# Six of the eight x pieces of the lower half asked for together, into landing tiles and idle sweep tiles

## The chip, the core and the metric

The kernel runs on one core of a Trainium2 chip. The metric is the device time of one execution in microseconds (us). TensorE does the matmuls, VectorE (DVE), ScalarE (ACT) and GpSimd (POOL) the elementwise work, and SyncE (SP) and ScalarE issue the DMAs, which run on 16 DMA engines that the queues share. Each engine works through its own instructions strictly in order.

## What is computed

One layer of a hybrid encoder on 2048 tokens of width 1024, all in float32. Only its first step, the combined input projection, is touched by the change:

```python
u = _rms_norm(h, norm_mix_g[l])
proj = u @ w_in[l]
hy = _short_conv_centred(proj[..., :HY_COLS], hy_conv_w[l], hy_conv_b[l])
...
qk = jax.nn.silu(_short_conv_centred(proj[..., HY_COLS:off], ml_conv_w[l], ml_conv_b[l]))
```

`h` is x here. The columns of `proj` are the input of the Hyena group (1536 columns, a long convolution by FFT), q and k of an mLSTM (1024), its v and output gate (1024) and its scalar gates (16). After both groups come an output projection, cross-attention into 256 memory tokens, a squared-ReLU MLP and a last norm.

## The kernel before

**Products.** A float32 operand is split into a high and a low part (`split`, L367: ScalarE casts the high part, VectorE subtracts it from the source to get the low one), and a product is made of three matmuls (`mm3`, L355). The left operand of the projection lives in two tiles for the whole stage: `xh` and `xl`, 128 partitions by 8 blocks of the width by 1024 tokens. That is one half of the tokens. There is one pair of these tiles, so the halves take turns in them.

**Pieces of x.** A half is two token chunks of 512, and a chunk is loaded in four pieces (c, j) of two width blocks: `x_load` (L517), 128 x 1024 elements each, from the transposed x, issued by SyncE into a landing tile of the tag "xn", of which there are two. `scaled` (L512) then does for a piece: two gains on VectorE (L510: times the norm's gain, times the row of inverse root mean squares `rb`), the cast into `xh` on ScalarE and the subtraction into `xl` on VectorE (L368). A chunk's `rb` is made by `diagonal` (VectorE, L496) and `spread` (a matmul with ones, L502, and a copy, L506). `x_chunk` (L524) is the generator that does this for one chunk, asking for piece j + 1 just ahead of `scaled` of piece j; `prep_x` (L639) chains the generators of both chunks of a half into `prepq`, and `pop` (L624) advances it by one piece.

**Who uses x.** Two kinds of passes over the weight columns, both 256 wide:

- `sweep` (L719) computes columns transposed, for the convolutions: each column block has two row tiles m and two token chunks, copies the products into a tile "P" (128 x 1088, two of them), convolves into a tile "cv" (the same size, two of them), and `sweep_out` (L789) transposes and stores the result.
- `natural` (L834) computes columns with the tokens on the partitions: for each weight tile eight row tiles t of 128 tokens. Row tiles 0 to 3 read token chunk 0 of the half, 4 to 7 chunk 1. It stores v and the sigmoid of o (L859) by ScalarE's queue (L860) and the gates by SyncE's (L865). It uses no "P" and no "cv".

**The order around the change.** `program` (L2019) lays out: sweeps 0 to 3 over half 0, then half 1 into `xh` and `xl` (`prep_x(1)`), sweeps 0 to 9 and `natural(1, (3, 0, 1, 2))` over half 1, then half 0 again (`prep_x(0)`, the "lower half" in what follows, since its rows come second), `natural(0, (3,))`, sweeps 4, 5, 8 and 9, and so on. Inside the last weight tile of `natural(1, ...)`, at row tile 4, `after()` sets `prepq`. From there on each row tile pops one piece: the four of chunk 0 in row tiles 4 to 7 of that weight tile (whose matmuls no longer read chunk 0), the four of chunk 1 in row tiles 0 to 3 of `natural(0, (3,))`, and its row tiles 4 to 7 need them.

The whole sequence is woven by `weave` with the generators of Hyena (`hyena`, L867), which run on TensorE between the projection's matmuls. In this stretch Hyena reads `a<-zg` (L935) and `a<-hy` (L938) by SyncE's queue, 1.5 MB for each step.

**Who sets the order on the engines.** The program text gives priorities and dependences. The order that each engine gets comes from a planner that simulates a time line (`schedule_with_timeline_sim`, L1988): it lets an instruction or a DMA go ahead of its place in the text when its inputs and its tile are free in the simulated time. The real engines then keep that order, so an instruction that waits holds everything behind it on its engine, and a DMA that waits holds everything behind it in SyncE's or ScalarE's queue.

Of the kernel before, what the change touches and what calls it, by code (L numbers as in the profile page):

```python
# [10 lines left out]
F32 = mybir.dt.float32  # L11
# [9 lines left out]
D = 1024  # L21
# [112 lines left out]
class Prog:  # L134
# [386 lines left out]
        self.nc.sync.dma_start(out=t, in_=src[:, 2 * j:2 * j + 2, 512 * c:512 * c + 512])  # L521
        return t

    def x_chunk(self, c):  # L524
        rb = self.spread(self.diagonal(self.rx[:, 4 * c:4 * c + 4]))
        xs = [self.x_load(c, 0)]
        for j in range(4):
            if j < 3:
                xs.append(self.x_load(c, j + 1))
            to = slice(2 * j, 2 * j + 2), slice(512 * (c % 2), 512 * (c % 2) + 512)  # L530
            self.scaled(xs.pop(0), 2 * j, self.g_mix, rb, *(t[(slice(None),) + to] for t in (self.xh, self.xl)))
            yield

    def x_first(self):
        nc, sb = self.nc, self.isb
# [101 lines left out]
        yield  # L637

    def prep_x(self, hf):  # L639
        self.prepq = chain(self.x_chunk(2 * hf), self.x_chunk(2 * hf + 1))  # L640

    def prep_mem(self):
        sb = self.isb
# [190 lines left out]
    def natural(self, hf, tiles, after=None, at=4):  # L834
        nc, a, sb = self.nc, self.a, self.isb
        xh, xl = self.xh, self.xl
        win = a["w_in"][0]
        for c2 in tiles:
            n = 256 if c2 < 3 else 272
            c0 = 2560 + 256 * c2  # L840
            wh, wl = next(self.wst)
            for t in range(8):
                if t % 4 == 0:
                    yield 11
                if t == at and c2 == tiles[-1] and after is not None:
                    after()
                ts = slice(128 * t, 128 * t + 128)
                r0 = 1024 * hf + 128 * t
                p = self.mm()
                for k in range(8):  # L850
                    self.mm3(p[:, :n], xh[:, k, ts], xl[:, k, ts], wh[:, k, :n], wl[:, k, :n], k == 0, k == 7)
                if self.pending:
                    self.pending.pop(0)()
                self.pop()
                so = sb.tile([128, 512], F32, tag="st", name="st", bufs=3)[:, 0:256]
                if c2 < 2:
                    nc.scalar.copy(so, p[:, :256])
                else:
                    nc.scalar.activation(so, p[:, :256], AF.Sigmoid)  # L859
                nc.scalar.dma_start(out=(self.d_vd if c2 < 2 else self.d_od)[r0:r0 + 128, 256 * (c2 % 2):256 * (c2 % 2) + 256],  # L860
                                  in_=so)
                if c2 == 3:
                    sg = sb.tile([128, 16], F32, tag="sg", name="sg", bufs=2)
                    nc.vector.tensor_tensor(sg, p[:, 256:272], self.gb, ALU.add)
                    nc.sync.dma_start(out=self.d_gt[r0:r0 + 128], in_=sg)  # L865
# [1130 lines left out]
def chain(*gens):  # L1996
    for g in gens:
        yield from g


def weave(a, b, wa, wb, until=False):
    da = db = 0.0
    fa = fb = False
    while not (fa and fb):
        if fb or (not fa and da / wa <= db / wb):
            try:
                da += next(a)
            except StopIteration:
                fa = True
        else:  # L2010
            try:
                db += next(b)
            except StopIteration:
                fb = True
                if until:
                    return


def program(p):  # L2019
    with ExitStack() as ms:  # L2020
        with ExitStack() as es:
            p.inproj_open(es)
            p.filters_open()
            p.prepq = p.x_first()
            p.pop()
            s = chain(p.sweep(range(4), 0, True, lambda: p.prep_x(1)), p.opened(), p.sweep(range(4), 1, False))
            f = p.filters()
            for _ in range(5):
                next(s)
            next(f)  # L2030
            next(f)
            next(s)
            weave(s, f, 140, 102, True)
            p.gates_open(es)
            n = p.memproj()
            m = p.mlstm(ms)
            with ExitStack() as hs:
                rest = chain(s, p.sweep(range(4, 10), 1, True), p.natural(1, (3, 0, 1, 2), lambda: p.prep_x(0)),
                             p.natural(0, (3,)), among(p.sweep((4, 5, 8, 9), 0, False), p.gates(), 2),
                             among(chain(p.natural(0, (0, 1)), p.sweep((6, 7), 0, False),  # L2040
                                         p.natural(0, (2,), p.prep_mem, 2)), p.states(), 1),
                             p.turned_in(), take(n, 2), beside_each(n, take(m, 6)))
                weave(rest, p.hyena(hs), 499, 297, True)
            for _ in rest:
                pass
        with ExitStack() as rs:
            p.ts = rs.enter_context(ExitStack())
            p.tail_open(p.ts)
            with ExitStack() as at:
                g = p.attention(at)  # L2050
                weave(g, m, 440, 96, True)
                ms.close()
                p.ffn_open(rs)
                for _ in g:
                    pass
            p.ffn()


def among(g, h, every):
    for i, v in enumerate(g):  # L2060
        yield v
        if i % every == every - 1:
            next(h, None)
    for _ in h:
        pass


def beside_each(g, h):
    for v in g:
        yield v  # L2070
        yield next(h, 0)
    yield from h


def take(g, n):
    for _ in range(n):
        v = next(g, None)
        if v is None:
            return
        yield v  # L2080
# [31 lines left out]
```

## Time and profile before

| | |
|---|---|
| median of 3 runs | 3120.02 us (3117.74 to 3126.49) |
| the profiled execution's own time | 3121.71 us |
| its span, first to last instruction | 3120.0 us |
| TensorE busy | 3025.7 us, 97% |
| mean granted TensorE clock | 0.988 |
| DMA moved | 607.07 MB, 195 GB/s on average |

All times of the trace are in microseconds from the span's start. A row of a timeline names the start, the length, the engine, the line, the operation, the tile written <- the tiles read, and in brackets the idle time before it and what ended it. SPq and ACTq are the DMA issues of SyncE and ScalarE. A row of a table of stretches gives, for each engine, its busy time and the number of instructions, then the granted TensorE clock (1.00 is full), the busy share of the DMA engines and what they moved. A list of waits names who waited for whom, the total in us, how many times, and the longest.

### The profile page before, as it was taken

How to read it: one execution, taken by the hardware profiler on the slowest of the kernel's cores; microseconds unless marked ns; L12 is line 12 of the kernel's file. 1: busy time of each engine (PE TensorE's matmuls, PEld its weight loads, DVE VectorE, ACT ScalarE, POOL GpSimd, SP SyncE). 2: the span in 40 equal slices, each digit the busy share in tenths (PEclk: the TensorE clock that was granted, in tenths of full speed). 3: DMA queues.
4: the chain of work that ended last, by engine and by line, in shares of the span. 5: the costliest groups of instructions: out<-in, count | busy, mean ns of one | idle time of the engine just before them, and what ended most of it. 6: DMA issues, size and time to landing. Idle time of an engine off the chain costs nothing.

```text
span 3120.0 us, 42912 instructions
## 1 busy us (share of the span) xinstructions
PE 3025.7 (97%) x14257; PEld 2374.8 (76%) x14257; DVE 1957.9 (63%) x3428; ACT 1498.4 (48%) x2930; POOL 1145.9 (37%) x802
## 2 busy tenths in 40 slices
PE   8999999989999898999999999999999999999998
PEld 6655667766677666888888888887888888888876
DVE  7865465446747356777665656657555686565696
ACT  6543465533646225555544455556455443333335
POOL 0122011200223243233142337766455475242693
PEclk9999999999999998999999999999999999999999
DMA  6554767676877996455375657656644565353434
GB/s 212 189 197 163 231 211 219 177 237 199 252 209 241 277 321 228 140 197 179 130 268 191 212 168 240 202 180 227 202 152 151 169 216 183 112 166 113 161 92 172
DMA packets 444102, 607.07 MB, mean 195 GB/s; under 512 B 38494, under 2 KB 248542, under 8 KB 442856
## 3 DMA queue, kind: packets, MB, share of 16 engines
q1 hardware_dynamic: 405988, 546.54, 54.3%
q10 hardware_dynamic: 37892, 57.79, 5.4%
q8 instruction: 113, 1.85, 0.2%
q14 instruction: 109, 0.89, 0.1%
HBM read 401.79 MB, written 202.41 MB: 194 GB/s over the span
## 4 chain that ended last, share of the span: by engine, by line
PE 55%; DVE 2%; issue 1%; DMA 1%; ACT 0%; POOL 0%; SPq 0%; ACTq 0%; POOLq 0%; DVEq 0%
PE mm L357 12%; PE mm L360 12%; PE mm L361 12%; PE hy L361 6%; PE hy L357 6%; PE hy L360 6%; DVE bl L1631 1%; PE hy L1287 1%; PE hy L1289 1%; DVE acc L1923 0%; PE hy L1534 0%; DVE acc L1957 0%; PE hy L1423 0%; DMA e<-hg 0%; PE hy L1249 0%
## 5 line engine op out<-in xcount | busy, mean ns | idle before, releaser
L1630 ACT CAST ah<-w 128x512 fp32r<-128x512 f32 x284 | 176.6, 622 | 304.8 <-PE hy L360 157.8
L1631 DVE TENSOR_TENSOR bl<-wr,bh 128x512 fp32r<-128x512 f32 x213 | 242.2, 1143 | 124.8 <-ACT bh L1630 124.2
L368 DVE TENSOR_TENSOR wl<-wn,wh 128x512 fp32r<-128x512 f32 (+1 forms) x300 | 220.6, 781 | 100.1 <-ACT wh L368 99.5
L998 POOL TENSOR_TENSOR b<-b,a 128x512 f32<-128x512 f32 x64 | 87.2, 1365 | 514.5 <-ACT b L996 215.4
L357 PE MATMUL mm<-xh,wh 128*128 128x512 f32 x640 | 267.5, 419 | 8.6 <-ACT wh L368 8.0
L360 PE MATMUL mm<-xl,wh 128*128 128x512 f32 x640 | 253.8, 397 | 1.3 <-DVE xl L368 1.3
L361 PE MATMUL mm<-xh,wl 128*128 128x512 f32 x640 | 255.0, 399 | 0.0
L1630 ACT CAST bh<-wr 128x512 fp32r<-128x512 f32 x232 | 143.5, 621 | 230.3 <-PE mm L361 173.1
L1631 DVE TENSOR_TENSOR al<-w,ah 128x512 fp32r<-128x512 f32 x236 | 216.8, 919 | 56.1 <-ACT ah L1630 56.0
L361 PE MATMUL mm<-bh,al 128*128 128x512 f32 x576 | 223.7, 391 | 2.6 <-POOL al L1631 2.6
L357 PE MATMUL mm<-bh,ah 128*128 128x512 f32 x576 | 225.6, 392 | 0.1
L360 PE MATMUL mm<-bl,ah 128*128 128x512 f32 x576 | 225.1, 391 | 0.0
L368 ACT CAST wh<-wn 128x512 fp32r<-128x512 f32 (+1 forms) x300 | 166.6, 618 | 113.9 <-PE mm L361 51.8
L360 PE MATMUL mm<-act,wh 128*128 128x512 f32 x512 | 200.6, 392 | 0.8 <-DVE act L368 0.8
L357 PE MATMUL mm<-act,wh 128*128 128x512 f32 x512 | 198.9, 394 | 1.4 <-ACT wh L368 1.3
L361 PE MATMUL mm<-act,wl 128*128 128x512 f32 x512 | 199.0, 392 | 0.0
L357 PE MATMUL hy<-bh,ah 128*128 128x512 f32 x448 | 175.2, 391 | 0.0
L360 PE MATMUL hy<-bl,ah 128*128 128x512 f32 x448 | 174.6, 390 | 0.0
L361 PE MATMUL hy<-bh,al 128*128 128x512 f32 x448 | 174.4, 390 | 0.0
L357 PEld LDWEIGHTS mm<-xh,wh 128*128 128x128 f32 x640 | 121.2, 190 | 60.9 <-issue 18.6
L357 PE MATMUL mm<-wh,xh 128*128 128x256 f32 (+1 forms) x512 | 155.2, 304 | 12.6 <-ACT xh L368 10.2
L361 PEld LDWEIGHTS mm<-xh,wl 128*128 128x128 f32 x640 | 121.0, 189 | 47.9 <-issue 23.2
(371 smaller groups left out, 8217.9 us busy)
## 6 DMA issues: line engine op xcount, KB each, us to landing
wr<-hc SPq DMA_DIRECT2D x224, 256.0 KB
w<-in_ff_w_dram SPq DMA_DIRECT2D x172, 256.0 KB
hc<-wn SPq DMA_DIRECT2D x128, 256.0 KB
wn<-in_w_in_dram SPq DMA_DIRECT2D x100, 256.0 KB
hc<-q SPq DMA_DIRECT2D x96, 256.0 KB
fs<-a SPq DMA_DIRECT2D x32, 512.0 KB
a<-fs SPq DMA_DIRECT2D x64, 256.0 KB
a<-zs SPq DMA_DIRECT2D x64, 256.0 KB
```

The source lines that it names most:

```text
L357: first = mm(ps, lh, rh, start=start, stop=False)
L360: mm(ps, lh, rl, start=False, stop=False)
L361: self.last = mm(ps, ll, rh, start=False, stop=stop)
L368: both = (self.nc.scalar.copy(hi, src), self.nc.vector.tensor_tensor(lo, src, hi.bitcast(F32), ALU.subtract))
L998: nc.gpsimd.tensor_tensor(xt, xt, hi[:, m], ALU.mult)
L1287: nc.tensor.matmul(dst, nm[:, h], va[:, h], start=True, stop=state is None)
L1289: nc.tensor.matmul(dst, rows_[d, 1][:, h], state[:, h], start=False, stop=True)
L1630: self.nc.scalar.copy(hi, src)
L1631: eng.tensor_tensor(lo, src, hi.bitcast(F32), ALU.subtract)
```

## The change

`x_chunk` and the chain of two are replaced by one generator over all eight pieces of a half, `x_chunks(hf)`. When it is called it first issues `deep` loads: two for half 1, six for half 0. Of the six the first two land in "xn" as before, and pieces 2 to 5 in tiles of the tags "P" and "cv", two of each. After each piece's `scaled` the load of the piece `deep` places further on is issued, into "xn": for half 0 these are the last two pieces. For half 1 a load now follows the `scaled` that frees its tile in the text, where it stood ahead of it, and the loads of the second chunk no longer stand behind that chunk's `spread`.

In `natural` the value `True` for `after` now stands for this generator: it is made (and so its loads are asked for) at row tile 0 of the last weight tile, and put into `prepq` at row tile 4, where the pieces began before. What is computed does not change, and neither does the number of loads, gains, casts and subtractions.

```diff
-    def x_chunk(self, c):
-        rb = self.spread(self.diagonal(self.rx[:, 4 * c:4 * c + 4]))
-        xs = [self.x_load(c, 0)]
-        for j in range(4):
-            if j < 3:
-                xs.append(self.x_load(c, j + 1))
-            to = slice(2 * j, 2 * j + 2), slice(512 * (c % 2), 512 * (c % 2) + 512)
-            self.scaled(xs.pop(0), 2 * j, self.g_mix, rb, *(t[(slice(None),) + to] for t in (self.xh, self.xl)))
-            yield
+    def x_chunks(self, hf):
+        parts = [(2 * hf + i, j) for i in range(2) for j in range(4)]
+        deep = 2 if hf else 6
+
+        def room(n):
+            if not 1 < n < deep:
+                return None
+            t = self.isb.tile([128, 1088], F32, tag=("P", "cv")[n % 2], name="xt", bufs=2)
+            return t[:, 0:D].rearrange("p (k t) -> p k t", k=2)
+
+        xs = [self.x_load(*parts[n], room(n)) for n in range(deep)]
+
+        def steps():
+            rb = None
+            for n, (c, j) in enumerate(parts):
+                if j == 0:
+                    rb = self.spread(self.diagonal(self.rx[:, 4 * c:4 * c + 4]))
+                to = slice(2 * j, 2 * j + 2), slice(512 * (c % 2), 512 * (c % 2) + 512)
+                self.scaled(xs.pop(0), 2 * j, self.g_mix, rb, *(t[(slice(None),) + to] for t in (self.xh, self.xl)))
+                if n + deep < 8:
+                    xs.append(self.x_load(*parts[n + deep]))
+                yield
+        return steps()
...
     def prep_x(self, hf):
-        self.prepq = chain(self.x_chunk(2 * hf), self.x_chunk(2 * hf + 1))
+        self.prepq = self.x_chunks(hf)
...
                 if t % 4 == 0:
                     yield 11
-                if t == at and c2 == tiles[-1] and after is not None:
-                    after()
+                if c2 == tiles[-1] and after is not None:
+                    if after is True and t == 0:
+                        nxt = self.x_chunks(0)
+                    if t == at:
+                        if after is True:
+                            self.prepq = nxt
+                        else:
+                            after()
...
-                rest = chain(s, p.sweep(range(4, 10), 1, True), p.natural(1, (3, 0, 1, 2), lambda: p.prep_x(0)),
+                rest = chain(s, p.sweep(range(4, 10), 1, True), p.natural(1, (3, 0, 1, 2), True),
```

## The prediction

> **What bounds the kernel now.** I began with the first part of the page, then read the list of who waited for whom on TensorE over the whole span (columns: who waited <- for whom; us in total, times, longest).
>
> ```profile
> span 3120.0 us, 42912 instructions
> PE 3025.7 (97%) x14257; PEld 2374.8 (76%) x14257; DVE 1957.9 (63%) x3428; ACT 1498.4 (48%) x2930; POOL 1145.9 (37%) x802
> ```
>
> ```profile
> PE mm L696 <- ACT o L686: 11.3, 2, 10.1
> PE mm L357 <- ACT xh L368: 10.2, 2, 7.4
> ```
>
> TensorE is busy for 97% of the span, so what can be won without removing matmuls are its gaps, 94.3 us in all. The second largest entry is the one that the change can reach: matmuls of L357 that wait for the cast of x (L368) twice, 7.4 us at the longest. Where this is, TensorE's timeline shows (start, us, engine, line, what, and in brackets the idle time before it and who ended it):
>
> ```profile
> 640.48 0.29 PE L357 MATMUL mm<-wh,xh 128*128 128x272 f32 x1
> ...
> 657.99 0.59 PE L191 MATMUL hy<-a,f 64*128 64x512 f32 x1
> 666.02 0.59 PE L357 MATMUL mm<-wh,xh 128*128 128x272 f32 x1 [7.44 <-ACT xh L368]
> ...
> 672.33 0.39 PE L357 MATMUL mm<-wh,xh 128*128 128x272 f32 x1 [0.86 <-DVE sg L864]
> ...
> 674.39 0.39 PE L361 MATMUL mm<-wh,xl 128*128 128x272 f32 x1 [0.24 <-DVE xl L368]
> ...
> 683.41 0.39 PE L357 MATMUL mm<-wh,xh 128*128 128x272 f32 x1 [2.72 <-ACT xh L368]
> ...
> 686.78 0.40 PE L357 MATMUL mm<-xh,wh 128*128 128x512 f32 x1
> ```
>
> The matmuls with 272 columns from 640.48 are the lower half's first weight tile, `natural(0, (3,))`. Its first four row tiles read token chunk 0, its last four chunk 1. TensorE stops at 658.58, when only chunk 1 is left to do. The four gaps sum to 7.44 + 0.86 + 0.24 + 2.72 = 11.26 us. Slices of 5 us there add the clock (columns: stretch; length and TensorE; weight load; VectorE; ScalarE; GpSimd; granted clock; DMA share; GB/s):
>
> ```profile
> 660.00:665.00 5.00, 0.00 (x0) 0.00 (x0) 0.87 (x2) 0.73 (x3) 0.00 (x0) 0.66 1.05 284
> 665.00:670.00 5.00, 3.98 (x14) 3.32 (x16) 3.75 (x5) 1.46 (x2) 0.00 (x0) 0.50 0.77 226
> 670.00:675.00 5.00, 3.90 (x21) 2.21 (x18) 2.66 (x6) 1.82 (x3) 0.00 (x0) 0.81 1.01 335
> ...
> 680.00:685.00 5.00, 2.28 (x16) 1.85 (x15) 2.64 (x3) 1.04 (x1) 0.00 (x0) 1.00 0.31 103
> ```
>
> After the 7.44 us gap the work ran at a clock of 0.50 and then 0.81: 3.98 x 0.50 + 3.90 x 0.19 = 2.7 us lost. After the 2.72 us gap it stayed at 1.00. So the switch costs 11.26 + 2.7 = 13.96 us, and that is the most to be won there.
>
> Why x is late, VectorE, ScalarE and SyncE's queue tell in turn:
>
> ```profile
> 631.85 2.73 DVE L510 SCALAR_TENSOR_TENSOR xt<-xt,par,rb 128x512 f32<-128x512 f32 x4
> ...
> 640.09 1.42 DVE L510 SCALAR_TENSOR_TENSOR xt<-xt,par,rb 128x512 f32<-128x512 f32 x2 [3.17 <-DMA xt<-in_x_t_dram]
> ...
> 645.09 2.49 DVE L368 TENSOR_TENSOR wl<-wn,wh 128x512 fp32r<-128x512 f32 x4
> ...
> 650.91 1.29 DVE L1013 TENSOR_TENSOR a<-hy,a 128x512 f32<-128x512 f32 x2 [1.80 <-DMA a<-hy]
> ...
> 657.60 1.41 DVE L510 SCALAR_TENSOR_TENSOR xt<-xt,par,rb 128x512 f32<-128x512 f32 x2 [4.33 <-DMA xt<-in_x_t_dram]
> ```
>
> ```profile
> 633.29 1.05 ACT L368 CAST xh<-xt 128x1024 fp32r<-128x1024 f32 x1 [0.53 <-DVE xt L510]
> ...
> 661.97 0.33 ACTq L860 DMA_DIRECT2D od<-st  x1
> 662.40 0.66 ACT L859 ACTIVATE st<-mm 128x256 f32<-128x256 f32 x2 [9.34 <-DMA a<-zg]
> ...
> 664.93 1.04 ACT L368 CAST xh<-xt 128x1024 fp32r<-128x1024 f32 x1 [1.87 <-DMA wn<-in_w_in_dram]
> ```
>
> ```profile
> 152.58 11.71 SPq L521 DMA_DIRECT2D xt<-in_x_t_dram  x4
> ...
> 635.74 1.59 SPq L521 DMA_DIRECT2D xt<-in_x_t_dram  x2
> ...
> 647.96 0.39 SPq L521 DMA_DIRECT2D xt<-in_x_t_dram  x1
> ...
> 648.90 2.22 SPq L935 DMA_DIRECT2D a<-zg  x2
> ...
> 656.60 0.37 SPq L521 DMA_DIRECT2D xt<-in_x_t_dram  x1
> ...
> 667.26 0.38 SPq L521 DMA_DIRECT2D xt<-in_x_t_dram  x1
> ...
> 674.37 0.38 SPq L521 DMA_DIRECT2D xt<-in_x_t_dram  x1
> ```
>
> Piece (0,2) of chunk 0 is 3.17 us late, under cover of other matmuls. Two things hold the first piece of chunk 1. Its load went out at 647.96, because both landing tiles ("xn") were full until then, and VectorE got it at 657.60. Its gain was done at 659.0, yet the cast came at 664.93: ScalarE stood 9.34 us at an `od` store (L860), behind the landing of Hyena's `a<-zg`, on DMA engines that were full (share 1.05). The later pieces come one by one behind each other's tiles: 656.60, 667.26, 674.37.
>
> **The change part by part.** *Six pieces at once.* Of the eight loads of the lower half, six go out from 635 on. The other two are among the four of 152.58, 480 us before VectorE takes them up at 631.85: the planner issues a load as soon as its tile is free, whatever the place in the program. So the two in "xn" don't move. Four pieces now land in the sweeps' "P" and "cv" tiles, and pieces 7 and 8 take the freed "xn" tiles, at 635.74, where (0,2) and (0,3) went before. The loads of 647.96, 656.60, 667.26 and 674.37 leave the crowded stretch.
>
> *What then paces the switch.* One piece costs VectorE 1.41 (two gains, 657.60) and 1.23 for xl (shortest, median and longest in ns):
>
> ```profile
> L368 DVE TENSOR_TENSOR xl<-xt,xh x8: 1212/1226/1226, 634.5 to 683.4; 128x1024 fp32r<-128x1024 f32 x8
> ```
>
> Eight pieces take 8 x 2.64 = 21.1 us; with 2.49 for the weights and 1.29 for Hyena, VectorE would be through at 631.85 + 24.9 = 656.7, before TensorE gets to 658.58. ScalarE needs 8 x 1.05 (633.29) = 8.4 us for the casts. So the data can be there in time; all 13.96 us are open to be won. The bounds of what stays: 0 where the casts stand ahead of the blocked store in ScalarE's order, and 6.0 where they stand behind it (worked out as the first rival). I take 2.0, nearer to 0: with data at hand the cast followed its gain after 0.53 us at 633.29, and the planner, to which x is now there, has no reason to put three stores ahead.
>
> *The clock.* It comes back with the gap. The rows say that 2.72 us keep it and 7.44 lose it. The Trainium skill, "TensorE: Matmul & The Clock Gate", Part 1, puts the limit at an idle window of about 3.4 us; both rows agree with it, and by it a remaining gap of 2 us would cost no clock.
>
> *The four loads in their new place.* "P" and "cv" come free when the last sweep of the upper half is written out:
>
> ```profile
> 483.28 1.26 DVE L773 SCALAR_TENSOR_TENSOR cv<-P,par,cv 128x1008 f32<-128x1008 f32 x1
> ...
> 510.95 0.60 SPq L832 DMA_DIRECT2D kn<-st  x1
> ...
> 490.00:515.00 25.00, 23.53 (x130) 17.22 (x129) 18.01 (x29) 19.01 (x32) 8.31 (x6) 1.00 0.93 284
> 515.00:535.00 20.00, 20.00 (x120) 15.98 (x119) 8.33 (x19) 9.59 (x20) 2.05 (x2) 1.00 0.42 115
> ...
> xt<-in_x_t_dram SPq DMA_DIRECT2D x6, 512.0 KB
> ```
>
> The first "P" is read for the last time at 484.5, the last `kn` store of the second "cv" goes out at 510.95. As the planner pulled the two loads of 152.58, I expect the four in 484 to 512, 120 us before their use. 4 x 0.524 MB at 284 GB/s are 7.4 us of DMA, in a stretch with a share of 0.93, ahead of one with 0.42. Lower bound 0: TensorE's gaps of 490 to 515 sum to 1.47 us, and the loads of a stage run ahead of it. Upper bound: four loads held SyncE's queue for 11.71 us at 152.58; held like that, and with the 7.4, what is behind them comes 19.1 us late. What that hold cost TensorE is seen in its waits from 140 to 180:
>
> ```profile
> PE hy L191 <- DVE b L338: 1.3, 1, 1.3
> PE mm L360 <- DVE xl L368: 1.3, 1, 1.3
> ```
>
> None of it is laid to a late load. I take 1.0. (The Trainium skill, "DMA: Bandwidth & Descriptors", Queues, rings and completion order, says that each DMA engine takes one queue's descriptors in ring order; by it, loads pulled ahead delay every SyncE load behind them by their whole 7.4 us, and the sum would come out 6.4 us higher. No row here shows which share of such a delay reaches TensorE.)
>
> *The upper half.* With two landing tiles its loads go out when "xn" is freed, as now; the loads of the second chunk only lose their place behind `spread`. The wait it has is the 1.3 us on xl above; VectorE's work sets it. 0, within -1.3 to +1.3.
>
> *The sweeps' tiles.* The lower half's first sweep needs "P" at 686.78, some 30 us after the gains are through; 0, covered by `natural`'s matmuls. Without that cover it would wait for one piece, 2.64.
>
> *The order of the rest.* The planner lays every engine's order anew. A single later wait can appear or vanish: up to 10.1 us (L696) either way. I take 0; what TensorE wins passes on, since the list has no later wait of that size but that one on ScalarE.
>
> The sum against the execution's own time, 3121.71: -13.96 + 2.0 + 1.0 = -10.96, so 3110.75. That execution lies 1.69 above the median of 3120.02; from the median it is **3109.1**.
>
> **The rivals.** *The store keeps ScalarE.* For it: 9.34 us behind `a<-zg`, on engines with a share of 1.05. Against it: 1.05 MB of x (647.96, 656.60) leave that stretch, 3.7 us at 284 GB/s. The cast then ends 3.7 us earlier, a gap of 3.7 stays, the 0.86 too, and half of the lost clock (1.35); the 0.24 and 2.72 go. That keeps 6.0 and wins 8.0; with the 1.0 it is 3113.0.
>
> *Slower: the pulled loads starve Hyena at 484 to 512.* For it: share 0.93 and the hold of 11.71. Against it: the quiet waits from 140 to 180, and 0.42 right behind. Its full price is 19.1, and 2.7 for a clock lost in such a gap: 21.8 against 13.96 won, +7.8, so 3127.9, or 3133.8 if the store keeps ScalarE too. It decides from some 14 us of lateness that no lead covers.
>
> *A new wait from the new order*, of the 10.1 us seen: 3119.2. For it: L696 and L686 have nothing to do with x, and such waits come from the order. Against it: only a few of that size in 3120 us. That the change doesn't do what it says (the pieces still go out one by one) would end near here as well, at 3120; against it speaks that the four tiles are free from 512 on.
>
> **How the numbers follow.** Forecast 0.50, its own range 3104 to 3115; the store 0.19; starved Hyena 0.16; new order, or no effect, 0.15. No change can be told from one within 0.3%, 9.4 us, that is 3110.7 to 3129.4. Faster: two thirds of the forecast (0.34), 0.03 of the store, 0.02 of an order that comes out better: 0.39. Slower: half of starved Hyena (0.08) and 0.05 of the new order: 0.13. The rest, 0.48, lies within. The range for 8 in 10 reaches from 3103 (all 13.96, the 1.3 and some of the order) to 3124 (the new order's case and the lighter half of the starved one).
>
> **What would show it.** Right: six x loads ahead of 635, four of them between 484 and 512, none between 640 and 675; TensorE's gaps between 655 and 690 below 3 us; a clock of 1.00 there; the first 512-column matmul of the next sweep near 675 rather than 686.78. The store rival: one gap of 3 to 4 us on xh and ScalarE idle behind a DMA. Starved Hyena: gaps at 490 to 520 with a DMA as the releaser. The forecast falls if the sweep begins before 680 and the end still doesn't move by 9 us, or if the x loads in "P" and "cv" go out only near 620.

## The result

| | before | after |
|---|---|---|
| median of 15 runs each | 3120.02 us | 3112.32 us (3108.30 to 3117.19) |
| the profiled execution's own time, its span | 3121.71, 3120.0 us | 3117.19, 3115.5 us |
| switch: first 272-column matmul to first 512-column matmul of the next sweep | 46.30 us | 36.76 us |

The ratio is 0.9974, with an interval of 0.9967 to 0.9981: 7.7 us are gone. The interval lies clear of 1, but the gain is inside the 0.3% that counts as no change. The forecast was 3109.1. In a later measurement of five rounds the same kernel came to 0.9965 (0.9952 to 0.9977).

The profile after. Lines from 850 on stand 20 lower in the code than before (the store of o, L860, is L880, the gates' add L884, the gates' store L885, Hyena's `a<-hy` L958), those around the memory projection 14. TensorE's list of waits first (us, times, longest), then its timeline at the switch:

```profile
PE mm L357 <- ACT xh L368: 1.3, 1, 1.3
```

```profile
641.36 0.29 PE L357 MATMUL mm<-wh,xh 128*128 128x272 f32 x1
...
662.07 0.29 PE L361 MATMUL mm<-wh,xl 128*128 128x272 f32 x1
663.65 0.39 PE L357 MATMUL mm<-wh,xh 128*128 128x272 f32 x1 [1.29 <-ACT xh L368]
663.88 0.28 PE L360 MATMUL mm<-wl,xh 128*128 128x272 f32 x1
666.11 0.69 PE L178 MATMUL hy<-a,f 64*128 64x512 f32 x1 [1.94 <-DVE a L1033]
...
678.12 0.40 PE L357 MATMUL mm<-xh,wh 128*128 128x512 f32 x1
```

Of the four gaps of before two are left, 1.29 and 1.94 us, with half a microsecond of work between them. The second is not on x itself: VectorE, held up by the same cast, subtracted `xl` late, and Hyena's product (L1033) stood behind that. VectorE's timeline shows it:

```profile
663.63 1.23 DVE L368 TENSOR_TENSOR xl<-xt,xh 128x1024 fp32r<-128x1024 f32 x1 [4.59 <-ACT xh L368]
664.77 1.28 DVE L1033 TENSOR_TENSOR a<-hy,a 128x512 f32<-128x512 f32 x2
```

Slices of 2 us (columns as in the prediction) give the clock:

```profile
666.00:668.00 2.00, 1.89 (x9) 1.14 (x10) 1.51 (x5) 0.59 (x1) 0.00 (x0) 0.90 1.00 336
668.00:670.00 2.00, 2.00 (x11) 2.00 (x11) 0.00 (x0) 0.39 (x1) 0.00 (x0) 0.50 1.06 394
670.00:672.00 2.00, 2.00 (x14) 2.00 (x14) 0.00 (x0) 0.00 (x0) 0.00 (x0) 0.75 1.02 373
```

Lost to it: 1.89 x 0.10 + 2.00 x 0.50 + 2.00 x 0.25 = 1.69 us. So 1.29 + 1.94 + 1.69 = 4.92 us of the 13.96 stay at the switch; 9.04 went. SyncE's queue and ScalarE show why (start, length; ACTq is a DMA issue of ScalarE):

```profile
484.50 0.39 SPq L521 DMA_DIRECT2D xt<-in_x_t_dram  x1
...
501.92 0.49 SPq L521 DMA_DIRECT2D xt<-in_x_t_dram  x1
...
503.73 0.37 SPq L521 DMA_DIRECT2D xt<-in_x_t_dram  x1
...
513.86 0.55 SPq L521 DMA_DIRECT2D xt<-in_x_t_dram  x1
...
640.70 0.39 SPq L521 DMA_DIRECT2D xt<-in_x_t_dram  x1
...
642.81 0.59 SPq L521 DMA_DIRECT2D xt<-in_x_t_dram  x1
```

```profile
650.43 0.33 ACTq L880 DMA_DIRECT2D od<-st  x1
650.79 1.05 ACT L368 CAST xh<-xt 128x1024 fp32r<-128x1024 f32 x1 [3.85 <-DMA a<-hy]
...
656.27 0.33 ACTq L880 DMA_DIRECT2D od<-st  x1
656.63 1.05 ACT L368 CAST xh<-xt 128x1024 fp32r<-128x1024 f32 x1 [3.57 <-DMA a<-hy]
...
662.19 0.33 ACTq L880 DMA_DIRECT2D od<-st  x1
662.55 1.04 ACT L368 CAST xh<-xt 128x1024 fp32r<-128x1024 f32 x1 [4.59 <-DMA a<-hy]
```

The loads did what was foretold: four at 484 to 514, none of the six after 643. But ScalarE's order now has one `od` store straight ahead of three of chunk 1's four casts. Each store holds ScalarE until one of Hyena's reads has landed, 3.85 + 3.57 + 4.59 us in all (in the second profile the middle one of the three is put down to VectorE's `xl`, 4.22 us), and the last cast comes at 662.55 for a TensorE that ran dry at 662.36.

In this one execution, the slowest of its 15, the lead at the sweep was 8.66 us (686.78 to 678.12), and 4.5 us at the end. Part of it was given back around 1010, where Hyena's inverse transform waited for VectorE:

```profile
1004.00 1.10 PE L971 MATMUL hy<-b,em 128*128 128x512 f32 x2 [1.27 <-DVE b L1019]
...
1012.38 2.08 PE L971 MATMUL hy<-b,em 128*128 128x512 f32 x2 [2.37 <-DVE b L1019]
```

In a second profile of the same kernel the same stretch has one such gap, of 1.11 us, and the span is 3107.7. The lead over before where the memory projection begins is 3.5 us in the first profile (1024.99 against 1028.53) and 9.1 in the second (1019.43). So that loss belongs to the execution, not to the change.

### The profile page after: what moved, and what is told of

It is laid out like the page before. It is cut to its first block, busy times and chain, and to the rows that moved or that the text cites. A ratio compares the mean times of both kernels' runs of the same rounds, so it can differ in the third digit from the quotient of the medians.

```text
span 3115.5 us, 42912 instructions
## 1 busy us (share of the span) xinstructions
PE 3024.1 (97%) x14257; PEld 2374.4 (76%) x14257; DVE 1946.3 (62%) x3428; ACT 1497.6 (48%) x2930; POOL 1144.0 (37%) x802
## 4 chain that ended last, share of the span: by engine, by line
PE 54%; DVE 3%; DMA 1%; issue 1%; ACT 1%; POOL 0%; SPq 0%; ACTq 0%; DVEq 0%; POOLq 0%
PE mm L357 12%; PE mm L360 11%; PE mm L361 11%; PE hy L361 5%; PE hy L357 5%; PE hy L360 5%; DVE bl L1651 1%; PE hy L1307 1%; PE hy L1309 1%; DMA w<-in_ff_w_dram 0%; DVE acc L1943 0%; PE hy L1554 0%; DVE acc L1977 0%; DMA h<-acc 0%; PE hy L1443 0%
```

## The experiments

What all of them say is easiest read from one number, the length of the switch. In the versions where TensorE never stops there it is 31.80 and 31.66 us; what is above that is gaps and lost clock. The lengths and gaps are each from one profile; each ratio is to runs of before that were measured beside it.

| kernel | switch, us | TensorE's gaps in it, us | time, us (runs) | ratio to before (interval) |
|---|---|---|---|---|
| before | 46.30 | 7.44, 0.86, 0.24, 2.72 | 3120.02 (15) | 1 |
| after | 36.76 | 1.29, 1.94 | 3112.32 (15) | 0.9974 (0.9967 to 0.9981) |
| after, second profile | 36.80 | 1.29, 1.94 | 3109.47 (1) | |
| after, five rounds | 38.08 | 0.26, 1.36, 1.94 | 3108.67 (5) | 0.9965 (0.9952 to 0.9977) |
| two loads ahead | 45.96 | 1.03, 6.49, 2.19 | 3119.99 (11) | 0.9997 (0.9987 to 1.0006) |
| four loads ahead | 38.64 | 3.81 | 3111.99 (1) | |
| loads held back to 600 | 38.46 | 2.08, 1.94 | 3109.14 (1) | |
| o store by GpSimd | 34.75 | 2.92 | 3106.89 (6) | 0.9961 (0.9947 to 0.9975) |
| o store by SyncE | 35.02 | 3.18 | 3107.53 (1) | |
| o store by GpSimd, two loads ahead | 43.60 | 0.85, 6.80, 1.04 | 3116.19 (12) | 0.9989 (0.9979 to 0.9998) |
| o and gate stores by GpSimd | 31.80 | none | 3107.93 (7) | 0.9963 (0.9950 to 0.9975) |
| the same, five rounds | 31.66 | none | 3105.28 (5) | 0.9948 (0.9934 to 0.9962) |

**Two loads ahead: is the gain the four pieces?** The new generator stays, without the sweeps' tiles.

```diff
-        deep = 2 if hf else 6
+        deep = 2
```

> The changed kernel with two loads ahead in both halves: one generator over both chunks and the new place of the call, but no piece in the sweeps' tiles. Theory (all of the gain is the four pieces in P and cv): loads one by one from 635 on, a gap of 6 to 8 us on xh near 659, the next sweep at 685 to 688, time 3120 within 3. Rival (the single generator, which no longer puts the second chunk's loads behind its spread, gives a part): the sweep at 681 to 684, time 3114 to 3117.

No gain is left: 0.9997. The loads go out one by one again and TensorE stops for x twice:

```profile
634.70 1.58 SPq L521 DMA_DIRECT2D xt<-in_x_t_dram  x2
...
644.67 0.61 SPq L521 DMA_DIRECT2D xt<-in_x_t_dram  x1
...
656.16 0.37 SPq L521 DMA_DIRECT2D xt<-in_x_t_dram  x1
...
663.43 0.37 SPq L521 DMA_DIRECT2D xt<-in_x_t_dram  x1
```

```profile
667.90 0.59 PE L357 MATMUL mm<-wh,xh 128*128 128x272 f32 x1 [6.49 <-ACT xh L368]
...
680.79 0.59 PE L357 MATMUL mm<-wh,xh 128*128 128x272 f32 x1 [2.19 <-ACT xh L368]
```

The first of the two gaps is not that of before, though it is nearly as long: chunk 1's first piece is cast at 654.33, and TensorE waits for the second, whose data VectorE got at 665.36. The merged generator, and the loads of the upper half's second chunk that no longer stand behind `spread`, are worth nothing that shows in the time; the four early pieces are the whole gain.

**Four loads ahead: do two pieces do it?**

```diff
-        deep = 2 if hf else 6
+        deep = 2 if hf else 4
```

> The changed kernel with four loads ahead in the lower half instead of six: one piece in P, one in cv, both of chunk 0. Theory (chunk 1's pieces are what TensorE waits for, and those two only were late under cover of other matmuls): pieces (1,0) and (1,1) go out at 640 to 643 instead of 648 and 657, (1,2) and (1,3) still one by one; the sweep begins between 678 and 683. Rival (any free landing tile is as good as another): half of the gain, 682.

Two loads go out at 484.94 and 504.16. The switch is 38.64 us, so two early pieces bring 7.7 of the 9.5 us that four bring, in the one run made; the sweep began at 679.43, inside the theory's range. The wait that is left is of another kind:

```profile
669.11 0.59 PE L357 MATMUL mm<-wh,xh 128*128 128x272 f32 x1 [3.81 <-DVE sg L884]
```

**Loads held back: what does the early place cost?** The four loads into "P" and "cv" are tied to the matmul ahead of them in the text, so that the planner can't pull them up.

```diff
-        self.nc.sync.dma_start(out=t, in_=src[:, 2 * j:2 * j + 2, 512 * c:512 * c + 512])
-        return t
+        d = self.nc.sync.dma_start(out=t, in_=src[:, 2 * j:2 * j + 2, 512 * c:512 * c + 512])
+        return (self.behind(d) if late else None, t)[1]
...
-        xs = [self.x_load(*parts[n], room(n)) for n in range(deep)]
+        xs = [self.x_load(*parts[n], room(n), 1 < n < deep) for n in range(deep)]
```

> The changed kernel with the four loads into P and cv tied in the planner's order behind the matmul ahead of them in the text, so that they go out near 610 instead of 484 to 514. Theory (the early place costs under 1 us): TensorE's gaps from 490 to 515 are back at 1.3 to 1.5 us from 1.3 to 2.2, the switch is as in the changed kernel (gaps of 1.3 and 1.9, the sweep at 676.9 to 678.1). Rival (pulled loads starve Hyena): the matmuls of 629 come 3 us or more earlier, and so does the sweep.

This kernel's SyncE queue, its slice of 490 to 515, and then the same slice of the changed kernel, in its first and in its second profile:

```profile
600.05 7.66 SPq L521 DMA_DIRECT2D xt<-in_x_t_dram  x4
```

```profile
490.00:515.00 25.00, 23.55 (x132) 17.35 (x131) 17.68 (x28) 19.08 (x33) 8.57 (x6) 1.00 0.93 283
```

```profile
490.00:515.00 25.00, 22.80 (x119) 15.79 (x118) 16.84 (x25) 18.05 (x31) 7.75 (x5) 1.00 0.92 278
```

```profile
490.00:515.00 25.00, 23.55 (x127) 16.88 (x126) 16.82 (x25) 17.97 (x30) 7.76 (x5) 1.00 0.93 287
```

TensorE is busy for 23.55 us of these 25 with the loads held back, and for 22.80 or 23.55 with them early; before it was 23.53. The early place costs 0 to 0.75 us; the 0.75 is one gap, which VectorE ended, in one of the three profiles of the changed kernel. The loads could wait until 600 just as well: the switch keeps its two gaps.

**The store of o by another queue: does it keep ScalarE?** In one kernel GpSimd issues the lower weight tile's `od` stores, in another SyncE (`nc.sync` in its place).

```diff
-                nc.scalar.dma_start(out=(self.d_vd if c2 < 2 else self.d_od)[r0:r0 + 128, ...],
+                (nc.gpsimd if hf == 0 and c2 == 3 else nc.scalar).dma_start(out=(self.d_vd if c2 < 2 else self.d_od)[r0:r0 + 128, ...],
```

> The changed kernel with the eight stores of the sigmoid of o in the lower half's first weight tile issued by GpSimd's queue instead of ScalarE's; TensorE's and VectorE's orders are the same, instruction by instruction. Theory (the store holds ScalarE): the four casts of chunk 1, which came at 650.8, 652.0, 656.6 and 662.6 behind three held stores, all come before 657; the gaps of 1.29 and 1.94 us between 655 and 680 go, the clock stays at 1.00, and the next sweep's first 512-column matmul comes at about 673.5 instead of 678.1 (1.29 + 1.94 + 1.4 for the clock). The end is 2 to 4.6 us earlier than the changed kernel's 3112.3, so 3107.7 to 3110.3. Rival (the data are late, x or Hyena's, on the full DMA engines): the gaps stay at 3 us or more under another releaser, the sweep still starts at 677 to 679, and the time is 3112 within 2.

> The same eight stores on SyncE's queue. Theory: ScalarE is free as with GpSimd's queue, but now a held store holds SyncE's loads of weights and of Hyena behind it; the sweep starts at 673.5 to 676, and a<-zg and a<-hy of the next step go out later than 665.3. Rival: no difference from the changed kernel, 678.

With GpSimd the order of TensorE's and VectorE's instructions stays as it was, and ScalarE's casts of chunk 1 run as soon as VectorE is through with the gains:

```profile
645.81 1.05 ACT L368 CAST xh<-xt 128x1024 fp32r<-128x1024 f32 x1
...
647.64 1.98 ACT L368 CAST xh<-xt 128x1024 fp32r<-128x1024 f32 x2
...
652.73 1.04 ACT L368 CAST xh<-xt 128x1024 fp32r<-128x1024 f32 x1
```

All four are done by 653.8, where the last began at 662.55. Both gaps on x are gone, and so is the loss of clock. What the store waited for was not data of its own: on GpSimd it waits for its sigmoid alone (the first of them; "ACT st" ends the idle time).

```profile
646.17 0.72 POOL L880 DMA_DIRECT2D od<-st  x1 [15.71 <-ACT st L879]
```

The time, 3106.89, is a little below the 3107.7 to 3110.3 expected. But the sweep does not begin at 673.5, because the next wait steps forward, in TensorE and in VectorE:

```profile
675.03 0.50 PE L357 MATMUL mm<-xh,wh 128*128 128x512 f32 x1 [2.92 <-DVE sg L884]
```

```profile
665.45 0.46 DVE L884 TENSOR_TENSOR sg<-mm,par 128x16 f32<-128x16 f32 x2 [5.67 <-DMA gt<-sg]
...
674.80 0.36 DVE L884 TENSOR_TENSOR sg<-mm,par 128x16 f32<-128x16 f32 x2 [8.29 <-DMA gt<-sg]
```

The gates of 128 tokens are added into a tile "sg", of which there are two (L883), and written out by SyncE's queue (L885). The add waits for an 8 KB store, and TensorE's next product needs the accumulator that the add reads. With SyncE the sweep begins at 675.29, as expected, behind 3.18 us on the same add; the next reads of Hyena go out from 665.37 there and from 663.33 with GpSimd.

**The o store moved, but two loads ahead: is the store enough by itself?** The edits of "two loads ahead" and "o store by GpSimd" together.

> The o stores on GpSimd's queue, but without the four early pieces (two loads ahead in both halves). It measures the store's hold by itself. Theory (two holds in series, the store and the late pieces, and each hides part of the other): the first cast of chunk 1 comes right behind its gains, at 658 to 660 instead of 664, the gap of 6.5 to 7.4 us shrinks to 1 to 3, but the gaps for the last pieces stay; the sweep begins at 679 to 683 instead of 685.4, and the time is 3114 to 3118. First rival (the store was the whole cause): the sweep by 676, time by 3110. Second rival (the pieces were the whole cause): 685, 3120.

The time, 3116.19, lies where the theory put it. The rest does not: the first gap did not shrink, and the sweep began at 684.26, nearer to the second rival's 685. The switch is 43.60 us against 45.96 with the store on ScalarE, 2.4 less. The first gap is as long as ever, since the data are late again:

```profile
669.26 0.60 PE L357 MATMUL mm<-wh,xh 128*128 128x272 f32 x1 [6.80 <-ACT xh L368]
```

```profile
666.72 1.41 DVE L510 SCALAR_TENSOR_TENSOR xt<-xt,par,rb 128x512 f32<-128x512 f32 x2 [6.31 <-DMA xt<-in_x_t_dram]
```

The 2.4 us come from the second gap, 1.04 instead of 2.19, and from the clock, which fell behind the longer of these two and not behind the shorter.

That each hold hides part of the other is not shown. In the new text the two gains nearly add up: the early pieces shorten the switch by 9.2 us with the store on ScalarE (45.96 to 36.76) and by 8.9 with it on GpSimd (43.60 to 34.75), moving the store by 2.4 without the early pieces and by 2.0 with them. In the kernel before, where the store did stand ahead of the cast that ended the first gap, the store was not moved alone.

**Both stores by GpSimd: full engines, or the queue's order?** The gate store could be slow because the DMA engines are full, or because it stands behind loads in SyncE's queue. The `od` edit and this one:

```diff
-                    nc.sync.dma_start(out=self.d_gt[r0:r0 + 128], in_=sg)
+                    (nc.gpsimd if hf == 0 else nc.sync).dma_start(out=self.d_gt[r0:r0 + 128], in_=sg)
```

> The kernel with the o stores on GpSimd's queue, and the lower half's eight small gate stores (8 KB each) on GpSimd's queue too, instead of SyncE's. With the o stores moved, VectorE waited 5.7 and 8.3 us for gate stores that stood behind loads, and TensorE 2.92 us for VectorE. Theory (the small store is slow because of what stands ahead of it in SyncE's queue): the 2.92 us go, the next sweep begins at 671.5 to 673 instead of 675.0, and the time is 3102 to 3106. Rival (the DMA engines are full, and a store of 8 KB takes 8 us on any queue): a gap of 2 to 3 us stays, the sweep begins at 674.5 to 676, the time is 3105 to 3109.

The waits of VectorE on the gate store, first with the store on SyncE (the o store by GpSimd), then on GpSimd (both stores); and the slices and TensorE's timeline of the latter:

```profile
DVE sg L884 <- DMA gt<-sg: 18.3, 4, 8.3
```

```profile
DVE sg L884 <- DMA gt<-sg: 5.9, 4, 2.2
```

```profile
660.00:665.00 5.00, 5.00 (x36) 4.09 (x36) 0.99 (x3) 0.97 (x2) 1.62 (x3) 1.00 1.08 355
665.00:670.00 5.00, 5.00 (x42) 5.00 (x41) 0.22 (x2) 0.77 (x2) 0.90 (x2) 1.00 1.05 415
```

```profile
671.79 0.40 PE L357 MATMUL mm<-xh,wh 128*128 128x512 f32 x1
```

The DMA engines are as full as with the o store alone on GpSimd, share 1.08 and 1.05, and the longest wait falls from 8.3 to 2.2 us. So it was the place in SyncE's queue and not the load of the engines alone. TensorE has no gap, the clock is 1.00, and the next sweep begins at 671.79, 6.3 us ahead of the changed kernel. The time did not follow: 3107.93 lies in the rival's range, not in the theory's, and the ratio, 0.9963, is no lower than that of the o store alone, 0.9961.

**The changed kernel again, and the fastest version beside it.** The first is one more run of the changed kernel, unchanged. The last two are five rounds each on one chip, against the same runs of before.

> The changed kernel once more, for a second profile. Its first profile was its slowest execution (3117.2 against a median of 3112.3). If the gain of the switch is given back by the order of the later work, the second profile shows the sweep at 678.1 and again only 3 to 4 us of lead left where the memory projection begins (1024.9 against 1028.4 before). If that was an accident of the one execution, the lead there is 7 to 8.5 us.

> The changed kernel beside the one with both stores on GpSimd's queue, on the same chip. Theory (what TensorE wins at the switch passes on to the end): the changed kernel at 3110 to 3114, and the one with both stores 4 to 6 us below it, as its sweep begins 5 to 6 us earlier (671.8 against 676.9 to 678.1). Rival (later stages that are bound by DMA take it back): less than 2 us between them.

> The kernel with the o stores and the gate stores of the lower half's first weight tile on GpSimd's queue. Theory: 3105 to 3109, no gap of TensorE between 640 and 700, clock 1.00 throughout. Rival: 3110 or more.

The gaps of 1.29 and 1.94 stand in both later profiles of the changed kernel too (1.36 in the third), so they belong to its order and not to one execution. With both stores on GpSimd it is 3105.28 against 3108.67, 3.4 us less, where the switch is 6.4 shorter. The intervals, 0.9934 to 0.9962 and 0.9952 to 0.9977, overlap a little: that it is faster is likely. The 3.4 lie between the theory's 4 to 6 and the rival's less than 2; how much of the 6.4 reaches the end is open. Of all kernels here it is the fastest.

## Why the prediction was right, and where it was not

**What was to be won: right.** 13.96 us were worked out for the switch from its gaps and its clock; 46.30 minus the 31.80 of a switch without a stop is 14.50.

**Six pieces at once: right for four, off for two.** The four went out at 484.50 to 513.86; 484 to 512 was read from the two loads of 152.58 and the tiles' last use. Pieces 7 and 8 went at 640.70 and 642.81 instead of 635.74. VectorE waits for no piece from 625 to 665 in any profile of the changed kernel.

**What then paces the switch: this term was mis-sized.** 2.0 us were to stay; 4.92 did, 1.29 + 1.94 of gaps and 1.69 of clock. The step that failed is the sentence that the planner, to which x is now there, "has no reason to put three stores ahead". It put one ahead of each of three casts, and each held ScalarE for 3.6 to 4.6 us; that the planner's simulated line knew nothing of these waits is my inference. The argument from VectorE's and ScalarE's own work (through by 656.7, casts of 8.4 us) was right as far as it went: with the `od` stores elsewhere the last cast ended at 653.8. What it left out is that an engine's order counts its DMA issues too. The first rival named the store, and its price, 6.0 kept and 3113.0 in all, is nearer to the measured 3112.32 than the forecast; the forecast's range holds both, so the time by itself does not tell them apart. Its form was another: not one gap of 3.7 after a long hold behind `a<-zg`, but three holds behind `a<-hy`, and a second gap handed on through `xl` and Hyena's product.

**The clock: wrong.** A gap of 2.72 that kept the clock was taken to say that 2 us cost none. Here 1.29 and 1.94 with half a microsecond between them halved it, and with two loads ahead a single gap of 2.19 did. The rule of the Trainium skill that I leaned on, "TensorE: Matmul & The Clock Gate", Part 1, speaks of an idle window of some 3.4 us. The traces agree with that length, but not with its use as a limit for one gap: what counted was how much idling fell into one step of a fixed grid (worked out in the last section). That the 2.72 us cost nothing before was luck of their place.

**The early loads: right to within 1 us.** 1.0 was taken, 0 to 0.75 measured. The starved Hyena falls: TensorE has no gap at 484 to 515 that a DMA ends, and holding the loads back to 600 wins nothing.

**Upper half, sweeps' tiles: right.** With two loads ahead the new text without the early pieces measures 0.9997, and TensorE has no gap between the next sweep's start and 700 in any of the three profiles of the changed kernel.

**The order of the rest: within what was allowed.** The give-back near 1010 in the first profile is of the kind allowed for, and did not come again. In the median 7.7 us reached the end, in the five rounds 10.9; both intervals hold the 9.5 by which the switch is shorter.

**The sum.** -13.96 + 4.92 + 0 to 0.75 gives -9.0 to -8.3; measured were -7.7 (interval -10.3 to -5.9) and, in the five rounds, 0.35% of 3122, -10.9 (-15.0 to -7.2). The forecast's -10.96 lies inside the second interval and just outside the first. That the five rounds come out at almost the forecast is luck, since the term for what stays at the switch was 2.9 us too small.

**What would show it.** Met: six x loads ahead of 635 (two of them at 152.56 to 164, as before), four at 484.50 to 513.86, within 2 us of what was said. Not met: no x load between 640 and 675 (two went, at 640.70 and 642.81), a clock of 1.00, and gaps below 3 us in all (3.23). The sweep began at 678.12, later than the 675 of the forecast. By the prediction's own words the forecast falls if the sweep begins before 680 and the end still does not move by 9 us. In the first measurement that is what happened, 678.12 and 7.7 us; in the five rounds the end moved by 10.9. Both intervals contain 9, so this sign is not decided.

## What to carry to other kernels

When an engine waits for late data, look at what stands between the data and the work in that engine's own order, its DMA issues above all: a store that waits for somebody else's landing holds back work whose data are there. Then look which wait ends last once that one is gone; here it was a gate store of 8 KB. A small store that frees a small tile does not belong in the queue that carries the big loads.

## What was not expected of the hardware

**The clock goes by the idle time in steps of 3.41 us, not by the longest gap.** Single gaps of 2.72 (before) and 2.92 us (o store by GpSimd) kept the clock at 1.00. One of 3.18 (o store by SyncE), one of only 2.19 (two loads ahead) and the pair of 1.29 and 1.94 lost it. Slices behind three of the single gaps, those of 2.92, 3.18 and 2.19 us in this order (the last gap ends at 680.79):

```profile
675.00:680.00 5.00, 4.97 (x22) 4.11 (x23) 2.87 (x7) 0.00 (x0) 0.42 (x1) 1.00 0.58 169
```

```profile
675.00:680.00 5.00, 4.71 (x14) 3.74 (x15) 1.85 (x6) 0.39 (x1) 0.00 (x0) 0.66 0.87 280
```

```profile
680.00:682.00 2.00, 1.21 (x5) 1.22 (x6) 1.23 (x1) 0.73 (x1) 0.00 (x0) 0.69 0.00 0
```

The traces show why. The clock is 1.00 or 0.50 at the switch, and within each of the traces all its changes lie whole multiples of 3.413 us apart, so each trace has a grid of such steps. Laid over TensorE's idle time, every step at full clock around the switch that held 1.87 us of idling or more was followed by 0.50, and every one with 1.86 or less was not; over the whole traces the border is less sharp, between 1.5 and 1.9. The 2.72 us before fell into two steps, as 1.40 and 1.32, and the 2.92 as 1.86 and 1.07; the 2.19 lay almost whole in one. The price comes in steps too. The low clock of the changed kernel lasted 3.4 us in its first two profiles and 6.8 in the third, which is why its switch took 36.76 us with 1.29 + 1.94 and 38.08 with 0.26 + 1.36 + 1.94. Nothing in these kernels sets where in the grid a gap falls.

**A store on ScalarE waits for a transfer that it does not need.** The same 128 x 256 `od` store waited 3.6 to 4.6 us on ScalarE's queue, by the profile for the landing of `a<-hy`, and for nothing but its sigmoid on GpSimd's. Why the one queue ties it to another's transfer the profile does not show; it stays open.

**A small store was late by its place in SyncE's queue more than by full DMA engines.** Between 655 and 670 the DMA share is 1.02 to 1.08 in both kernels. With the o store by GpSimd the gates added at 648.36 were issued by SyncE only at 658.18, and the store issued at 665.80 held its tile until the next add at 674.80, 9.0 us later:

```profile
665.80 1.25 SPq L885 DMA_DIRECT2D gt<-sg  x2
```

With both stores by GpSimd the gates added at 648.07 were issued at 648.51, and the eight stores took from issue to landing:

```profile
DMA to landing us min/median/max: 2.9/4.9/7.0
```

So SyncE's order alone held the first of these stores back by 9.8 us, and on full engines 8 KB still needed up to 7.0 us. The Trainium skill, "DMA: Bandwidth & Descriptors", Queues, rings and completion order, says that each DMA engine takes turns between the queues and works one queue off in ring order; the landing in 9.0 us behind loads and in 7.0 at most without them agrees with it.
